# Order of the S5 output products inside a slot of a two-layer decoder trunk

## The chip, the cores and the metric

The kernel runs on one core of a Trainium2 chip. The metric is the device time of one execution in microseconds (us). Three runs of the kernel before gave 893.55, 893.63 and 894.71 us; their median, 893.63 us, is the time before. One further execution was profiled, and every row shown here is from that one.

Engine names are those of the profile: PE is TensorE's matmul side and PEld its weight loads, DVE is VectorE, ACT ScalarE, POOL GpSimd, and SP the queue that issues most transfers. SPq, ACTq and POOLq are the queues that issue DMAs.

## The reference

The reference is a causal decoder trunk of two layers over 256 positions of width 2048, in float32. Each layer is a normalisation, a large input projection, two kinds of sequence mixer side by side, a gate, and an output projection; a last normalisation follows. The first layer mixes with dilated attention and gated linear attention (GLA), the second with an S5 state-space layer and a gated linear recurrence (HGRN2).

What matters here is S5. Its 1024 channels are 64 groups of 16, each with a complex diagonal state of 64:

```
bu_re = einsum('gph,sbgh->sbgp', bb_re, ut);  bu_im = einsum('gph,sbgh->sbgp', bb_im, ut)
x_re, x_im = associative_scan over the positions, with the decay a_re, a_im
y = einsum('ghp,sbgp->bsgh', c_re, x_re) - einsum('ghp,sbgp->bsgh', c_im, x_im) + d_skip * ug
y = gelu(y);  return y * sigmoid(y @ w_glu + b_glu)
```

## The kernel before

**The projections.** Almost all of the time is weight projections. Each weight block of 512 columns comes from memory in groups of 1 MB (`raw`, three buffers, line 144). `load_split` (line 143) splits each half group into a rounded part `wh` on ACT (line 168) and a remainder `wl` on DVE (line 169), with three buffers each. `gemm_fm` (line 181) and `gemm_tm` (line 200) then issue three products for every 128 rows: high by high, high by low, low by high. A half group is 24 matmuls of 256 columns, or 12 of 512. The loads, `wh` and `wl` have raised priority.

**Slots.** After each half group `hook()` (line 135) takes one entry of the list `fillq` and issues its functions directly behind the last projection matmul. So S5's small matmuls stand between the half groups of the HGRN2 projections. S5 is done in four quarters (`s5_quarter`, line 552), each with eleven slots (line 651): two slots of input products with the scan, some empty ones, one in which the next quarter's input is loaded, and two slots of output products.

**A quarter.** `v_mm` (line 574) issues the input products: 64 rows by 64 columns, for two halves `g` of the partitions (matmul line 583). DVE multiplies them with tables (lines 589 to 592), scans (lines 603 and 604), and writes two results: the tile `X` (line 611, one instruction for each half `g`) and then the tile `t2`, which is `t["t"][1]` (line 612). `y_mm` (line 614) makes the output in one bank `py` of PSUM. For each of eight channel pairs `pr` there are two products over 128 rows of `X` with the tables `PA` and `PB` (line 621), and two over 64 rows of `t2` with `Pi` (line 625), which add into columns 1 to 63 of the same targets. The half `g` goes to partitions 64 g to 64 g + 63. A float32 product is two matmul instructions in the trace, so a slot of four pairs is 16 products and 32 instructions, 16 from each line. `finish` (line 631) copies `py` out on ACT (line 633), sends it to memory and back in another layout (lines 636 and 639; four of the eight writes are issued by ACT, four by POOL), and applies the gelu (lines 641 to 649).

**What sets the order.** The program is written in one order, and a planner with a model of the engines' times (`schedule_with_timeline_sim=True`, line 1124) turns it into a fixed order for each engine ahead of the run. It may place an instruction between others when its inputs come late in the model. Products into one PSUM bank stay in the order of the program. On the chip each engine takes its list in order and waits on semaphores. `SP` issues the `raw` loads and the loads of `X` from one queue (lines 157 and 567); `X` has two buffers, so a new load of `X` waits until line 621 has read the old one.

Of the kernel before, what the change touches and what calls it, by code (L numbers as in the profile page):

```python
# [57 lines left out]
def trunk(ctx: ExitStack, tc: tile.TileContext, I, out):  # L58
    nc = tc.nc
    V, G, A, T = nc.vector, nc.gpsimd, nc.scalar, nc.tensor  # L60
# [29 lines left out]
    def pm_tile(name="pm"):  # L90
        return pm.tile([128, 512], F32, name=name, tag="pm")
# [162 lines left out]
    gs = small.tile([128, 8], F32, name="gs")  # L254
# [297 lines left out]
    def s5_quarter(qt):  # L552
        t = {}
# [20 lines left out]
        def v_mm(h, n):  # L574
            def go():
                if n == 0:
                    t["pv"] = pm_tile().rearrange("p (w r c) -> p w r c", w=2, r=4)
                pv, X = t["pv"], t["X"]
                for w in range(2):
                    for pr in range(2 * n, 2 * n + 2):  # L580
                        for g in range(2):
                            us = slice(64 - g * 64, 128 - g * 64)
                            T.matmul(pv[g * 64:g * 64 + 64, w, pr], t["W"][w][us, 4 * h + pr],
                                     X[us, g, 4 * h + pr], start=True, stop=True)
                if n == 1:
                    hs = slice(4 * h, 4 * h + 4)
                    Rc, Rs, _ = t["R"]
                    t1, t2, t3, t4 = t["t"]
                    V.tensor_mul(t1[:, hs], pv[:, 0], Rc[:, hs])
                    V.tensor_mul(t4[:, hs], pv[:, 0], Rs[:, hs])  # L590
                    V.tensor_mul(t2[:, hs], pv[:, 1], Rs[:, hs])
                    V.tensor_mul(t3[:, hs], pv[:, 1], Rc[:, hs])
            return go
# [17 lines left out]
                V.tensor_sub(t["X"][gs, g, :, 1:64], t1[gs, :, 0:63], t3[gs, :, 0:63])  # L611
            V.tensor_add(t2, t2, t4)

        def y_mm(pr):
            def go():
                if pr == 0:
                    t["py"] = pm_tile().rearrange("p (r c) -> p r c", r=8)
                py, X = t["py"], t["X"]
                PA, PB, Pi = t["P"]
                for g, w in enumerate((PA, PB)):  # L620
                    T.matmul(py[g * 64:g * 64 + 64, pr], w[:, pr], X[:, g, pr], start=(pr == 0), stop=False,  # L621
                             skip_group_check=True)
                for g in range(2):
                    gs = slice(g * 64, g * 64 + 64)
                    T.matmul(py[gs, pr, 1:64], Pi[gs, pr], t["t"][1][gs, pr, 0:63], start=False, stop=True,  # L625
                             skip_group_check=True)
                if pr == 7:
                    finish()
            return go

        def finish():
            ys = sp_.tile([128, 8, 64], F32, name="ys")
            A.activation(ys, t["py"], AF.Copy)
            for g in range(2):
                for s in range(4):
                    (nc.gpsimd if s % 2 else nc.scalar).dma_start(
                        yv[g, s][:, 8 * qt:8 * qt + 8], ys[g * 64 + s * 16:g * 64 + s * 16 + 16])
            yc = sp_.tile([128, 2, S], F32, name="yc")
            nc.gpsimd.dma_start(yc, s5_y[256 * qt:256 * qt + 256].rearrange("(j p) f -> p j f", p=128))
            gw = sp_.tile([128, 2, S], F32, name="gw")  # L640
            A.activation(gw, yc, AF.Square)
            A.activation(gw, gw, AF.Copy, scale=0.044715, bias=1.0)
            V.tensor_mul(gw, gw, yc)
            A.activation(gw, gw, AF.Tanh, scale=math.sqrt(2.0 / math.pi))
            A.activation(yc, yc, AF.Copy, scale=0.5)
            for n in range(2):
                V.scalar_tensor_tensor(oT[:, 2 * qt + n].rearrange("p (c s) -> p s c", s=4),
                                       gw[:, n].rearrange("p (s c) -> p s c", s=4), 1.0,
                                       yc[:, n].rearrange("p (s c) -> p s c", s=4), op0=OP.add, op1=OP.mult)

        return load0, [[load1, v_mm(0, 0), v_mm(0, 1)], [v_mm(1, 0), v_mm(1, 1), scan], [], [], None, [], [], []] + [[y_mm(4 * n + m) for m in range(4)] for n in range(2)] + [[]]

    quarters = [s5_quarter(qt) for qt in range(4)]
    quarters[0][0]()
    for qt in range(4):
# [94 lines left out]
    for half in range(2):  # L750
# [8 lines left out]
        for g in range(2):  # L759
# [3 lines left out]
            for n in range(2):  # L763
                k0 = 8 * g + 4 * n
                if half:
                    w, l = xh[:, k0:k0 + 4], xl[:, k0:k0 + 4]
                else:
                    w = stream.tile([128, 4, 256], F32R, name="wh", bufs=3)
# [368 lines left out]
```

## Time and profile before

| | |
|---|---|
| median of three runs | 893.63 us (893.55 to 894.71) |
| the profiled execution | 892.18 us, of which its span, first to last instruction, is 890.4 us |
| PE busy | 874.7 us, 98% of the span, 7728 matmuls |
| DVE, ACT busy | 635.5 us (71%), 472.0 us (53%) |
| mean granted clock of TensorE | 0.995 of full speed |

A busy share is an average over the whole span. Matmuls are pipelined, so the end of one is modelled and the starts are the firmer numbers: the time that a run of matmuls takes is read from the start of its first to the start of what follows it.

### The profile page before, as it was taken

The page shows a single profiled execution, that of the slowest core. Times are in us where ns is not written, and L with a number is a line of the kernel's source. Part 1 is how long each engine was busy: PE and PEld are TensorE (multiplying, and loading weights), DVE is VectorE, ACT ScalarE, POOL GpSimd, SP SyncE. Part 2 cuts the span into 40 slices and gives each one's busy share as a digit, 9 for nine tenths or more (in the row PEclk, how much of TensorE's full clock was granted, in tenths as well). Part 3 has the DMA queues.
Part 4 walks back from the last instruction along what each step waited for, and adds up shares of the span by engine and source line. Part 5 has one row for each costly group of instructions (what it writes and reads, how often), then busy time and mean ns, then how long its engine had stood idle before and what let it go on. Part 6 is the DMA issues. An engine that isn't in the chain of part 4 may idle for free.

```text
span 890.4 us, 18689 instructions
## 1 busy us (share of the span) xinstructions
PE 874.7 (98%) x7728; PEld 802.0 (90%) x7728; DVE 635.5 (71%) x1197; ACT 472.0 (53%) x715; POOL 54.4 (6%) x106
## 2 busy tenths in 40 slices
PE   8999999999999999999999999999999999999995
PEld 8987899889998899999999998799877899988894
DVE  7988975989869858756675677676987756665562
ACT  7654546665645765645543335355545475444451
POOL 0001100111101101000000001100110000000000
PEclk9999999999999999999999999999999999999998
DMA  9827743777656555555576566744643544544532
GB/s 317 316 102 218 259 160 146 237 256 251 220 204 230 205 190 196 197 200 199 200 283 222 206 230 198 260 172 167 225 166 139 206 190 172 202 180 177 179 132 94
DMA packets 40388, 180.40 MB, mean 203 GB/s; under 512 B 12720, under 2 KB 14256, under 8 KB 22768
## 3 DMA queue, kind: packets, MB, share of 16 engines
q1 hardware_dynamic: 29440, 154.99, 49.2%
q0 software_dynamic: 7984, 22.69, 7.5%
q10 hardware_dynamic: 2880, 1.54, 0.6%
q8 instruction: 60, 0.98, 0.4%
q14 instruction: 24, 0.20, 0.1%
HBM read 166.48 MB, written 12.71 MB: 201 GB/s over the span
## 4 chain that ended last, share of the span: by engine, by line
PE 81%; DVE 6%; DMA 4%; ACT 4%; issue 3%; SPq 0%; POOL 0%; ACTq 0%; POOLq 0%; DVEq 0%
PE pg L181 47%; PE pg L200 24%; DMA raw<-in_w_dram 2%; PE pg L756 2%; DVE wl L169 2%; PE pm L287 1%; PE pm L339 1%; DMA E<-ed 1%; ACT wh L168 1%; PE pm L621 1%; PE pm L625 1%; PE pm L308 1%; PE pm L415 1%; PE pm L1025 1%; ACT bb L1019 0%
## 5 line engine op out<-in xcount | busy, mean ns | idle before, releaser
L168 ACT ACTIVATE wh<-raw 128x1024 fp32r<-128x1024 f32 (+2 forms) x276 | 287.7, 1046 | 325.4 <-PE pg L181 193.7
L169 DVE TENSOR_TENSOR wl<-raw,wh 128x1024 fp32r<-128x1024 f32 (+2 forms) x276 | 332.0, 1206 | 167.9 <-ACT wh L168 163.1
L181 PE MATMUL pg<-xh,wh 128*128 128x256 f32 x1024 | 161.8, 279 | 2.2 <-ACT wh L168 2.2
L181 PE MATMUL pg<-xh,wl 128*128 128x256 f32 x1024 | 163.2, 280 | 0.4 <-DVE wl L169 0.4
L181 PE MATMUL pg<-xl,wh 128*128 128x256 f32 x1024 | 161.2, 278 | 0.0
L181 PEld LDWEIGHTS pg<-xh,wh 128*128 128x128 f32 x1024 | 136.7, 188 | 3.8 <-ACT wh L168 3.2
L181 PEld LDWEIGHTS pg<-xh,wl 128*128 128x128 f32 x1024 | 137.0, 188 | 1.6 <-DVE wl L169 0.8
L181 PEld LDWEIGHTS pg<-xl,wh 128*128 128x128 f32 x1024 | 136.7, 188 | 0.6 <-issue 0.3
L200 PE MATMUL pg<-wl,xh 128*128 128x512 f32 x320 | 100.9, 396 | 0.6 <-DVE wl L169 0.6
L200 PE MATMUL pg<-wh,xl 128*128 128x512 f32 x320 | 100.7, 394 | 0.0
L200 PE MATMUL pg<-wh,xh 128*128 128x512 f32 x320 | 100.2, 394 | 0.0
L200 PEld LDWEIGHTS pg<-wl,xh 128*128 128x128 f32 x320 | 59.0, 188 | 14.2 <-DVE wl L169 1.4
L200 PEld LDWEIGHTS pg<-wh,xl 128*128 128x128 f32 x320 | 59.8, 188 | 12.8
L200 PEld LDWEIGHTS pg<-wh,xh 128*128 128x128 f32 x320 | 59.3, 188 | 12.8
L181 PE MATMUL pg<-yh,wh 128*128 128x256 f32 x320 | 50.0, 277 | 0.0
L181 PE MATMUL pg<-yl,wh 128*128 128x256 f32 x320 | 49.5, 277 | 0.0
L181 PE MATMUL pg<-yh,wl 128*128 128x256 f32 x320 | 49.5, 277 | 0.0
L181 PEld LDWEIGHTS pg<-yh,wh 128*128 128x128 f32 x320 | 42.6, 188 | 0.0
L181 PEld LDWEIGHTS pg<-yl,wh 128*128 128x128 f32 x320 | 42.4, 188 | 0.0
L181 PEld LDWEIGHTS pg<-yh,wl 128*128 128x128 f32 x320 | 42.4, 188 | 0.0
L965 POOL DMA_DIRECT2D tabs<-pc x44 | 23.8, 547 | 162.3 <-DVE x L975 42.5
L200 PE MATMUL pg<-wh,yh 128*128 128x512 f32 x96 | 30.1, 395 | 0.0
(350 smaller groups left out, 1008.2 us busy)
## 6 DMA issues: line engine op xcount, KB each, us to landing
raw<-in_w_dram SPq DMA_DIRECT2D x100, 1024.0 KB, 4.9
raw<-in_wo_dram SPq DMA_DIRECT2D x28, 1024.0 KB, 4.8
tb<-tabs POOLq DMA_DIRECT2D x8, 768.0 KB, 6.9
tabs<-pc POOLq DMA_DIRECT2D x20, 256.0 KB, 5.5
raw<-in_wg_dram SPq DMA_DIRECT2D x4, 1024.0 KB, 4.8
raw<-in_wo1l_dram SPq DMA_DIRECT2D x4, 1024.0 KB, 4.8
raw<-in_w_dram SPq DMA_DIRECT2D x6, 512.0 KB, 7.9
tabs<-pc POOLq DMA_DIRECT2D x24, 128.0 KB, 4.6
```

Source lines behind the costliest of these rows:

```text
L168: state["wh"] = A.activation(w, r, AF.Copy)
L169: V.tensor_sub(l, r, w)
L181: state["mm"] = T.matmul(ps[:, c], w[:, cs], a[:, kt], start=(i == 0 and n == 0 and c % 2 == 0), stop=(i == last and n == 2), skip_group_c ...
L200: state["mm"] = T.matmul(ps[:, t], a[:, kt, ts_], w, start=(i == 0 and n == 0), stop=(i == last and n == 2), skip_group_check=True)
L287: T.matmul(ps[32 * b:32 * b + 32, t, hd], k[:, hd, r], Q[:, hd, r], start=True, stop=True)
L308: T.matmul(ps[j0:j0 + h, hd, j0 + h:j0 + 2 * h], k[:, hd, b:b + h], Qp[:, hd, b + h:b + 2 * h], start=True, stop=True)
L339: T.matmul(ps[:, (hd - h0) * dv:(hd - h0 + 1) * dv], AT[:, hd, t + j], v[:, j, hd * dv:(hd + 1) * dv], start=(j == 0), stop=(j == t))
L415: T.matmul(ps[:, t, 0:n], q[:, t * 128:(t + 1) * 128], k[:, 0:n], start=True, stop=True)
L621: T.matmul(py[g * 64:g * 64 + 64, pr], w[:, pr], X[:, g, pr], start=(pr == 0), stop=False, skip_group_check=True)
L625: T.matmul(py[gs, pr, 1:64], Pi[gs, pr], t["t"][1][gs, pr, 0:63], start=False, stop=True, skip_group_check=True)
L756: T.matmul(ps[:, t, 0:256], a_[:, kt, ts_], w_, start=(kt == 0 and n == 0), stop=(kt == KT - 1 and n == 2), skip_group_check=True)
L965: nc.gpsimd.dma_start(tabs[qt, dst, n], t[src].rearrange("p a b -> p (a b)"))
```

## The change

In a slot of the output, the eight products over 128 rows are issued first, for all four channel pairs, and then the eight over 64 rows. Before, the two kinds took turns, pair by pair. Products, operands, targets and start and stop flags are the same, and a slot's list now has one function in place of four.

```diff
-        def y_mm(pr):
+        def y_mm(n):
             def go():
-                if pr == 0:
+                if n == 0:
                     t["py"] = pm_tile().rearrange("p (r c) -> p r c", r=8)
                 py, X = t["py"], t["X"]
                 PA, PB, Pi = t["P"]
-                for g, w in enumerate((PA, PB)):
-                    T.matmul(py[g * 64:g * 64 + 64, pr], w[:, pr], X[:, g, pr], start=(pr == 0), stop=False,
-                             skip_group_check=True)
-                for g in range(2):
-                    gs = slice(g * 64, g * 64 + 64)
-                    T.matmul(py[gs, pr, 1:64], Pi[gs, pr], t["t"][1][gs, pr, 0:63], start=False, stop=True,
-                             skip_group_check=True)
-                if pr == 7:
+                for pr in range(4 * n, 4 * n + 4):
+                    for g, w in enumerate((PA, PB)):
+                        T.matmul(py[g * 64:g * 64 + 64, pr], w[:, pr], X[:, g, pr], start=(pr == 0), stop=False,
+                                 skip_group_check=True)
+                for pr in range(4 * n, 4 * n + 4):
+                    for g in range(2):
+                        gs = slice(g * 64, g * 64 + 64)
+                        T.matmul(py[gs, pr, 1:64], Pi[gs, pr], t["t"][1][gs, pr, 0:63], start=False, stop=True,
+                                 skip_group_check=True)
+                if n == 1:
                     finish()
             return go
...
-        return load0, [[load1, v_mm(0, 0), v_mm(0, 1)], [v_mm(1, 0), v_mm(1, 1), scan], [], [], None, [], [], []] + [[y_mm(4 * n + m) for m in range(4)] for n in range(2)] + [[]]
+        return load0, [[load1, v_mm(0, 0), v_mm(0, 1)], [v_mm(1, 0), v_mm(1, 1), scan], [], [], None, [], [], []] + [[y_mm(0)], [y_mm(1)], []]
```

## Rows read from the trace of the kernel before

**Rows 1.** The page: busy time and share of each engine, the clock that TensorE was granted in 40 slices of the span (9 is 90% or more), and the shares of the chain of work that ended last, by engine.

```profile
PE 874.7 (98%) x7728; PEld 802.0 (90%) x7728; DVE 635.5 (71%) x1197; ACT 472.0 (53%) x715; POOL 54.4 (6%) x106
...
PEclk9999999999999999999999999999999999999998
...
PE 81%; DVE 6%; DMA 4%; ACT 4%; issue 3%; SPq 0%; POOL 0%; ACTq 0%; POOLq 0%; DVEq 0%
```

**Rows 2.** The view of waits, PE alone, over the whole span: who waited for whom, us in total, times, the longest.

```profile
PE pg L181 <- ACT wh L168: 2.2, 3, 0.9
...
PE pg L200 <- DVE wl L169: 0.6, 2, 0.3
```

**Rows 3.** The same view from 500 to 700 us, for ACT.

```profile
ACT wh L168 <- PE pg L181: 47.9, 23, 4.0
ACT wh L168 <- PE pg L200: 20.3, 11, 4.4
```

**Rows 4.** The groups of instructions, shapes kept apart: line, engine, operation, tiles, rows * columns of the array, shape, count | busy us, mean ns of one | idle before.

```profile
L621 PE MATMUL pm<-X,tb 128*64 128x64 f32 x128 | 11.4, 246 | 0.0
L625 PE MATMUL pm<-t,tb 64*64 64x63 f32 x128 | 10.6, 242 | 0.0
...
L621 PEld LDWEIGHTS pm<-X,tb 128*64 128x64 f32 x128 | 6.7, 134 | 3.5 <-issue 1.4
...
L1025 PEld LDWEIGHTS pm<-PP,bb 128*64 128x64 f32 x128 | 4.2, 138 | 1.3 <-ACT wh L168 0.7 <-ACT junk L344 0.3
```

**Rows 5.** The timeline of PE in the first output slot of the first quarter: start us, us, engine, line, operation, tiles, rows * columns, shape, count of neighbours merged into the row. The rows left out go on in turns.

```profile
527.46 0.34 PE L621 MATMUL pm<-X,tb 128*64 128x64 f32 x4
527.73 0.33 PE L625 MATMUL pm<-t,tb 64*64 64x63 f32 x4
527.99 0.34 PE L621 MATMUL pm<-X,tb 128*64 128x64 f32 x4
...
529.31 0.33 PE L625 MATMUL pm<-t,tb 64*64 64x63 f32 x4
529.57 0.74 PE L181 MATMUL pg<-xh,wh 128*128 128x256 f32 x4
```

**Rows 6.** The timeline of PE at two places where small matmuls of one shape stand in a row: 32 of S5's table products over 128 rows (line 1025, in the preparation), and 32 and 64 of its input products over 64 rows (line 583), each with the projection matmuls behind them.

```profile
150.86 1.15 PE L1025 MATMUL pm<-PP,bb 128*64 128x64 f32 x32
151.94 0.39 PE L181 MATMUL pg<-xh,wl 128*128 128x256 f32 x1
...
503.12 1.15 PE L583 MATMUL pm<-X,tb 64*64 64x64 f32 x32
504.19 0.74 PE L181 MATMUL pg<-xh,wh 128*128 128x256 f32 x4
...
616.16 2.08 PE L583 MATMUL pm<-X,tb 64*64 64x64 f32 x64
618.18 0.75 PE L181 MATMUL pg<-xh,wl 128*128 128x256 f32 x4
```

**Rows 7.** The timeline of PE at the beginning of the output slots of the second, third and fourth quarter, where other work stands between the first products.

```profile
566.28 0.34 PE L621 MATMUL pm<-X,tb 128*64 128x64 f32 x4
...
567.86 0.33 PE L625 MATMUL pm<-t,tb 64*64 64x63 f32 x4
...
633.40 0.33 PE L621 MATMUL pm<-X,tb 128*64 128x64 f32 x2
...
634.42 0.27 PE L625 MATMUL pm<-t,tb 64*64 64x63 f32 x2
...
657.10 0.33 PE L621 MATMUL pm<-X,tb 128*64 128x64 f32 x2
...
659.18 0.33 PE L625 MATMUL pm<-t,tb 64*64 64x63 f32 x4
```

**Rows 8.** The timeline of DVE: the instruction that writes `t2` (line 612) in each of the four quarters.

```profile
522.19 0.68 DVE L612 TENSOR_TENSOR t<-t,t 128x512 f32<-128x512 f32 x1
...
563.77 0.69 DVE L612 TENSOR_TENSOR t<-t,t 128x512 f32<-128x512 f32 x1
...
632.34 0.69 DVE L612 TENSOR_TENSOR t<-t,t 128x512 f32<-128x512 f32 x1
...
656.28 0.68 DVE L612 TENSOR_TENSOR t<-t,t 128x512 f32<-128x512 f32 x1
```

**Rows 9.** The timeline of PE: the two places between 500 and 740 us at which a projection waited for `wl`, with the wait and its releaser in brackets; and the half group before the first of them.

```profile
554.65 0.62 PE L200 MATMUL pg<-wl,xh 128*128 128x512 f32 x2
...
557.78 0.72 PE L200 MATMUL pg<-wl,xh 128*128 128x512 f32 x2 [0.21 <-DVE wl L169]
...
648.64 0.73 PE L200 MATMUL pg<-wl,xh 128*128 128x512 f32 x2 [0.34 <-DVE wl L169]
```

**Rows 10.** The timelines of DVE and ACT around these places: the `wl` of 554.65 us; the first table product of the fourth quarter, with DVE's wait before it; and ACT's two waits for the transfer of `yc`.

```profile
553.25 1.20 DVE L169 TENSOR_TENSOR wl<-raw,wh 128x1024 fp32r<-128x1024 f32 x1
...
638.94 0.42 DVE L589 TENSOR_TENSOR t<-pm,tb 128x256 f32<-128x256 f32 x1 [1.49 <-PE pm L583]
...
550.90 0.64 ACT L641 ACTIVATE gw<-yc 128x512 f32<-128x512 f32 x1 [1.05 <-DMA yc<-s5y]
...
649.87 0.63 ACT L641 ACTIVATE gw<-yc 128x512 f32<-128x512 f32 x1 [1.59 <-DMA yc<-s5y]
```

**Rows 11.** The view of waits from 500 to 700 us, for the queue of SP.

```profile
SPq L567 <- PE pm L621: 12.5, 2, 7.4
```

## The prediction

> **What bounds the kernel now.** I read the page first. PE is busy for 98% of the span, DVE for 71%, ACT for 53%, and the chain of work that ended last is PE for 81% [rows 1]. Next the view of waits: over the whole span PE waits 2.2 us for ACT's `wh` in one kind of projection and 0.6 us for DVE's `wl` in the other [rows 2]. Seen from the other side, between 500 and 700 us, where all output slots lie, ACT waits 34 times and 68.2 us in all for PE to give back a buffer of `wh` [rows 3]: the supply of weights is mostly ahead of PE. So PE's own list is the bound, and a microsecond taken out of it should leave the total. The clock is granted in full in nearly every slice [rows 1], so no gain is to be looked for there.
>
> Then the timeline of PE in one output slot. The reader is to see how regular it is: the groups of four instructions from line 621 and of four from line 625 follow each other without a pause in the profile's busy time, and the next projection matmul begins at 529.57 us after a beginning at 527.46 us, 2.11 us for 32 instructions [rows 5]. That is 0.264 us for each of eight groups. Where 32 small matmuls of one shape stand in a row, they take 1.08 us over 128 rows (150.86 to 151.94 us) and 1.07 us over 64 rows (503.12 to 504.19 us); 64 of them take 2.02 us [rows 6]. The same number of instructions of the same size costs twice as much when the shape changes after every fourth. The mean durations hide this (246 and 242 ns, [rows 4]), since matmuls overlap; only the distance of starts shows it.
>
> **The change, part by part.** *The price of one turn.* From 32 to 64 instructions of one shape is 0.95 us, so a further instruction in a row costs 0.95 / 32 = 0.030 us [rows 6]. Four cost 0.12 us, and a group of four with its change of shape costs 0.264 us [rows 5]: a turn costs 0.145 us.
>
> *The new slot.* It is one group of 16 over 128 rows and one of 16 over 64. A group of 16 is bounded from two sides: a group of four with its turn plus twelve more instructions, 0.264 + 12 x 0.030 = 0.62 us, or the 32 in a row less sixteen, 1.07 - 16 x 0.030 = 0.59 us. Two groups are 1.18 to 1.24 us, and the slot gets 0.87 to 0.93 us shorter. I take 0.88, near the first, since its group of four is these very instructions. It is also six turns fewer at 0.145 us.
>
> *Eight slots.* There are 128 instructions from each of the two lines [rows 4], 32 in a slot, so eight slots: 8 x 0.88 = 7.0 us, and 7.0 to 7.4 by the two bounds. The places where other work stands between the first products need a count of their own [rows 7]. Before, the second quarter has the four instructions of the first pair alone and the other fourteen groups or so later; the third and fourth have the first product of half 0 alone, and the rest later. Counted as groups of one shape the quarters have 16, 16, 17 and 17, together 66. With the new order each needs four, and the third and fourth probably one more, because the first product waits for one half of `X` and the others for both: 18. So 48 turns go, 48 x 0.145 = 7.0 us, the same as by slots.
>
> *The wait for `t2`.* The first product over 64 rows now stands behind eight products over 128 rows, not behind two. PE reaches it some 12 x 0.030 = 0.36 us later after the slot's beginning, and `t2` has been there before: its instruction ended at 522.87, 564.46, 633.03 and 656.96 us [rows 8], and line 625 began at 527.73 [rows 5], 567.86, 634.42 and 659.18 us [rows 7], that is 4.9, 3.4, 1.4 and 2.2 us later. No new stall is expected; if the cover went, the whole rest of PE's list would be queued behind line 625. I cost this at nothing.
>
> *What is moved on other engines.* No instruction and no transfer is added. SP waits 12.5 us in two waits for line 621 before it may load a new `X` [rows 11], and the `raw` loads stand behind it in the same queue. Since line 621 now ends before the last products of line 625, SP goes on 0.6 us before the slot ends, and earlier by what the slots have saved. ACT's copy of `py` waits for the last product of line 625, which stays last. So both are released earlier, never later.
>
> *What does not come along.* Two places are tight already. At 557.78 and 648.64 us PE waits 0.21 and 0.34 us for `wl`, and the `wl` that ended at 554.45 us (553.25 + 1.20) was used at 554.65 us [rows 9, 10]. Ahead of them DVE works off the scan of a quarter between the splits, and PE reaches them 1.76 us earlier (two slots) than before. DVE starts these scans when the input products of the quarter are done, which also move. At the later place DVE was waiting 1.49 us for these products [rows 10] and can use no more than that, so 1.76 - 1.49 = 0.27 us comes back as a wait of PE. The other thing in the way is ACT: it stands 1.05 and 1.59 us for the transfer of `yc` [rows 10] ahead of the next `wh`. That transfer starts from the end of the output slots, so it moves too, unless its queue is held by `raw` loads. If it did not move at all, ACT would stand there 1.76 us longer, and with 0.20 us of cover at 554.65 us PE would lose up to 1.6 us in each of the two places, 3.2 us in all; at the lower end nothing. I take a give-back of 0.3 us, near the lower end, as the first cause alone has a row for its size.
>
> *The sum.* 7.0 - 0.3 = 6.7 us less. For a profiled execution that is 892.18 - 6.7 = 885.5 us with a span of 883.7. The median of three runs stands 1.45 us above the profiled execution, and the difference carries over: 893.63 - 6.7 = 886.9 us.
>
> **Rivals.**
>
> *The supply takes part of it.* As bounded above, the transfer of `yc` may not come earlier, and DVE, which is nearly always busy around the two waits, may end first there. That gives back up to 3.2 + 0.3 = 3.5 us and a time of 890.1 us. For it: the waits of rows 9. Against it: 68.2 us of ACT waiting for PE in the same stretch [rows 3].
>
> *The groups are cut up again.* The planner may put other work of another shape between the products, or the order may not survive into PE's list. Then the turns stay and the time is 893.6 us. Against it: in all four quarters the products of a slot stand in the program's order in the trace before, and apart from their beginnings they are in one piece [rows 5, 7].
>
> *The planner moves the output slots ahead of the scan (slower).* The plan is made anew from a changed program. If the slots of every quarter were placed two half groups earlier relative to DVE's scan, PE would arrive 5.8 us earlier (a half group is 2.9 us, from 554.65 to 557.78 us less the wait of 0.21 [rows 9]), and against the covers of 4.9, 3.4, 1.4 and 2.2 us it would wait 0.9 + 2.4 + 4.4 + 3.6 = 11.3 us: 893.63 - 7.0 + 11.3 = 897.9 us. With one half group it is 1.5 + 0.7 = 2.2 us of waits and a time of 888.8. It is slower than before from between one and two half groups on. For it: in two quarters the cover is small. Against it: the number and size of the instructions in a slot do not change, so a model of their times has little reason to move a slot that far.
>
> *Weight loads that don't overlap (slower).* Eight products over 128 rows in a row load weights into the same rows of the array each time. If a load had to wait for the matmuls in flight, a pair would cost 134 + 246 = 380 ns [rows 4], a slot 8 x 0.38 + 0.61 = 3.65 us in place of 2.11, and the time would be 893.63 + 8 x 1.54 = 905.9 us. Against it: line 1025 has the same shape in a row, and its 32 loads of 138 ns [rows 4], 4.4 us together, stand within 1.08 us [rows 6]; they must overlap. The Trainium skill has such a rule, in "TensorE: Matmul & The Clock Gate", Part 3, "The mechanism": a weight load overlaps matmuls in flight only when its group of rows differs. By that rule this rival would be the forecast; by the rows of line 1025 it is not.
>
> **How the numbers follow.** What a measurement of this kernel can tell from no change is about 0.2%, 1.8 us. My forecast has a chance of 0.70. The supply rival has 0.15, and it is faster by more than 1.8 us over its whole stretch. The planner's rival has 0.03 with one half group, still faster, and 0.04 with two, slower. Loads that don't overlap have 0.02, slower. Groups cut up again have 0.06, no change. So faster 0.70 + 0.15 + 0.03 = 0.88, the same 0.06, slower 0.06. The forecast's own range is 886.2 (7.4 us, nothing given back) to 887.8; the low end goes to 885.4, since the two waits of rows 9 (0.55 us) could go too if the plan falls well, and the high end to 890.6, which takes in the supply rival and leaves out about 0.12.
>
> **What would show it right or wrong.** In the timeline of PE an output slot must have two groups, of 16 instructions each, and take 1.18 to 1.24 us from the first of line 621 to the projection matmul behind it. The busy time of PE must fall by about 6 to 7 us with its share near 98%. The waits of PE for `wl` should be 0.6 to 1 us in total; 3 us or more there, or under the transfer of `yc` in ACT's waits, is the supply rival. A wait of PE at line 625 for line 612 is the planner's. If a slot stays at 2 us with the groups in the new order, the price of a turn, which I take from other lines of the same shapes, is wrong, and the prediction with it.

## The result, and the profile after

The changed kernel takes 889.11 us (median of 20 runs, 885.8 to 894.61) beside 894.5 us for the kernel before (median of 20 runs too, one of them an outlier of 3954.35 us that a median hardly feels). The medians are 5.4 us apart. The ratio is 0.9936 with an interval of 0.9922 to 0.9951, that is 5.7 us less, with 4.4 to 7.0 us inside the interval. The forecast was 6.7 us less and 886.9 us. The sign is right, the time lies inside the range, and 0.9 us of the 2.2 us between forecast and median come from the kernel before, whose median is 894.5 us here against 893.63 us when the forecast was made.

The slots first. The timeline of PE in the second output slot of the first quarter, columns as in [rows 5]:

```profile
533.77 0.50 PE L181 MATMUL pg<-xh,wl 128*128 128x256 f32 x3
534.21 0.69 PE L622 MATMUL pm<-X,tb 128*64 128x64 f32 x16
534.82 0.68 PE L627 MATMUL pm<-t,tb 64*64 64x63 f32 x16
535.43 0.74 PE L181 MATMUL pg<-xh,wh 128*128 128x256 f32 x4
```

Two groups of 16 instead of eight of four [rows 5], and from 534.21 to the projection behind at 535.43 us it is 1.23 us. (Lines 622 and 627 are the 621 and 625 of before; everything behind them has moved by two.) The other unbroken slots take the same 1.226 us. Summed over every stretch of output products in the four quarters, from the start of the matmul ahead of a stretch to the start of the matmul behind it, it is 19.61 us before and 12.58 us after: 7.04 us less. (Without the steps into the stretches it is 17.09 and 10.06 us, 7.03 us less.)

The page of the profiled execution nevertheless says that its span is longer, 892.7 us against 890.4:

```profile
PE 874.1 (98%) x7728; PEld 804.5 (90%) x7728; DVE 636.0 (71%) x1197; ACT 473.1 (53%) x715; POOL 54.4 (6%) x106
...
PEclk9999999999999999999999999999999999999998
...
PE 74%; DVE 8%; ACT 6%; DMA 5%; issue 5%; SPq 0%; POOL 0%; POOLq 0%; DVEq 0%; ACTq 0%
```

PE's busy time fell by 0.6 us, not by 6 to 7 [rows 1]. This execution is the longest of the 20 (894.61 us), so its span alone says nothing; it has to be cut at a point that both kernels pass. The first input product of S5 (line 583) is such a point: nothing that the change touches stands before it, and up to there PE, ACT, DVE and POOL do the same instructions in the same order in both traces. Before, it begins at 503.12 us [rows 6]. After:

```profile
509.86 0.86 PE L583 MATMUL pm<-X,tb 64*64 64x64 f32 x22
```

It begins 6.74 us later, in a stretch that the change does not touch. From there to the end it is 890.4 - 503.12 = 387.28 us before and 892.7 - 509.86 = 382.84 us after: 4.44 us less. So in this execution 7.04 us went from the slots and 2.6 us came back behind them. The view of waits, PE over the whole span, shows the larger part (columns as in [rows 2]):

```profile
PE pg L200 <- ACT wh L168: 1.8, 1, 1.8
...
PE pg L200 <- DVE wl L169: 0.4, 2, 0.2
```

The single wait of 1.8 us for `wh` is new in this kind of projection. With the waits for `wl` it makes 2.2 us, against 0.6 before [rows 2]: 1.6 us come back here. It stands just ahead of the fourth quarter's slots. The timelines of PE, ACT and POOL around it:

```profile
653.78 0.62 PE L200 MATMUL pg<-wl,xh 128*128 128x512 f32 x2
656.17 0.74 PE L200 MATMUL pg<-wh,xh 128*128 128x512 f32 x2 [1.77 <-ACT wh L168]
```

```profile
644.81 1.06 ACT L672 ACTIVATE gk<-gf 128x1024 f32<-128x1024 f32 x1
645.78 1.99 ACT L168 ACTIVATE wh<-raw 128x1024 fp32r<-128x1024 f32 x2
653.88 0.63 ACT L643 ACTIVATE gw<-yc 128x512 f32<-128x512 f32 x1 [6.11 <-DMA yc<-s5y]
655.08 1.99 ACT L168 ACTIVATE wh<-raw 128x1024 fp32r<-128x1024 f32 x2
```

```profile
640.01 2.15 POOL L638 DMA_DIRECT2D s5y<-ys  x4
650.87 0.72 POOL L641 DMA_DIRECT2D yc<-s5y  x1 [8.72 <-DMA s5y<-ys]
```

ACT does two `wh` and then stands 6.11 us for `yc`; the next `wh` starts at 655.08 and PE, which needs it, goes on at 656.17. In the trace before the same wait of ACT was 1.59 us [rows 10], and three `wh` stood between the writes of `y` and that wait, not two. POOL's own queue before:

```profile
639.36 2.15 POOL L636 DMA_DIRECT2D s5y<-ys  x4
646.83 0.72 POOL L639 DMA_DIRECT2D yc<-s5y  x1 [5.32 <-DMA s5y<-ys]
```

From POOL's first write of `y` to the load of `yc`, which waits for all the writes to land, it is 10.86 us instead of 7.47. In the second traces below it is 11.35 and 7.99 us.

The remaining 1.0 us is in the projections themselves. The start-to-start distance of line 181's matmuls has two values in these traces, and each holds for long stretches. The timeline of PE at 760 us, before and then after:

```profile
760.02 0.62 PE L181 MATMUL pg<-xl,wh 128*128 128x256 f32 x4
760.47 0.62 PE L181 MATMUL pg<-xh,wl 128*128 128x256 f32 x4
```

```profile
759.95 0.63 PE L181 MATMUL pg<-xl,wh 128*128 128x256 f32 x4
760.42 0.64 PE L181 MATMUL pg<-xh,wl 128*128 128x256 f32 x4
```

Four matmuls take 0.453 us in the one and 0.471 us in the other, 113.4 and 117.8 ns each, at the same granted clock of 1.00. Summed over the 1211 steps of line 181 behind the first input product, what lies over 113.4 ns is 0.95 us before and 1.95 us after. With that the stretch adds up to the 0.1 us in which spans and waits are given: -7.04 + 1.6 + 1.0 = -4.4 us. Ahead of the first input product the same sum is 1.96 us before and 6.98 us after, which is 5.0 of the 6.74 us by which this execution came late to S5.

### The profile page after: what moved, and what is told of

It reads as the page before. It is cut to its first block, busy times and chain, and to the rows that moved or that the text cites. A ratio compares the mean times of both kernels' runs of the same rounds, so it can differ in the third digit from the quotient of the medians.

```text
span 892.7 us, 18688 instructions
## 1 busy us (share of the span) xinstructions
PE 874.1 (98%) x7728; PEld 804.5 (90%) x7728; DVE 636.0 (71%) x1197; ACT 473.1 (53%) x715; POOL 54.4 (6%) x106
## 4 chain that ended last, share of the span: by engine, by line
PE 74%; DVE 8%; ACT 6%; DMA 5%; issue 5%; SPq 0%; POOL 0%; POOLq 0%; DVEq 0%; ACTq 0%
PE pg L181 48%; PE pg L200 17%; DVE wl L169 2%; PE pg L758 2%; DMA tabs<-pc 2%; ACT wh L168 1%; PE pm L287 1%; DMA E<-ed 1%; PE pm L339 1%; DMA s5y<-ys 1%; ACT bb L1021 1%; DMA raw<-in_w_dram 1%; ACT x L1039 1%; PE pm L308 1%; DVE PP L1005 1%
## 5 line engine op out<-in xcount | busy, mean ns | idle before, releaser
L181 PE MATMUL pg<-xl,wh 128*128 128x256 f32 x1024 | 163.8, 280 | 0.0
```

The lines of the kernel that those rows point to most:

```text
L181: state["mm"] = T.matmul(ps[:, c], w[:, cs], a[:, kt], start=(i == 0 and n == 0 and c % 2 == 0), stop=(i == last and n == 2), skip_group_c ...
```

## The experiments

Times are medians beside runs of the kernel before on the same chip. "The stretch" is the time from the first input product to the end of the span in the profiled execution: 387.28 us before, 382.84 us after.

**The changed kernel and the kernel before, a second trace of each.** No edit.

> The changed kernel once more, for a second trace. Both theories of the price (change of shape, or adding into a target just written) expect output slots of 1.23 us and a time 0.5 to 0.8% below before. Theory A of the trace: the steps between the projection matmuls of line 181 have two rhythms, 113.4 and 117.8 ns, drawn anew in each execution; then this trace has slow stretches at other places or of another total length, and time less 4.4 ns for every slow step is within 2 us of the first trace's (about 894.6 - 8.1 = 886.5 us). Theory B: the changed order brings them; then the long slow stretches from 365 to 464 us and from 744 to 788 us stand there again. The wait of 1.8 us for ACT in the fourth quarter: if it comes from the transfer of yc landing late in that one execution, it is gone or has another size; if the plan makes it, it is there again with 1.5 to 2 us.

> The kernel before once more, for a second trace. Slots of 2.10 us. If the wait of PE in the fourth quarter belongs to the changed kernel, PE waits under 0.5 us there, as in the first trace (0.34), and ACT waits under 2 us for the transfer of yc of the third quarter (1.59). If the slow rhythm of line 181 from 742 to 787 us, which stands in all five traces with a changed order, belongs to them too, it is missing here; if it is drawn by lot, it may stand here.

The changed kernel: 889.68 us, ratio 0.9919 (0.9887 to 0.9951). The slots take 1.226 us again. The wait of PE for `wh` is there again, 2.29 us, behind a wait of ACT for `yc` of 6.64 us, so it belongs to the changed kernel's plan and not to one execution. The slower rhythm between 365 and 464 us, 99 us long in the first trace, is gone, and the one between 742 and 788 us is there again. The stretch is 384.84 us: here the fourth quarter's slots themselves came out longer, under a clock that fell soon behind the end of the wait at 652.72 us. Windows of that trace: start:end, us, busy time of PE (count), PEld, DVE, ACT, POOL, then granted clock, DMA share, GB/s.

```profile
652.00:653.00 1.00, 0.28 (x1) 0.28 (x2) 0.75 (x2) 1.00 (x2) 0.00 (x0) 1.00 0.34 139
653.00:655.00 2.00, 2.00 (x26) 1.43 (x25) 2.00 (x4) 2.00 (x4) 0.00 (x0) 0.88 0.00 0
655.00:656.00 1.00, 1.00 (x7) 0.45 (x6) 1.00 (x2) 0.61 (x1) 0.00 (x0) 0.50 0.00 0
656.00:659.00 3.00, 3.00 (x51) 2.68 (x51) 2.18 (x6) 0.26 (x1) 0.00 (x0) 0.68 0.62 224
```

0.50 is the lower of the two levels, 1.2 of 2.4 GHz. The last 48 products of the quarter take 2.69 us there and 1.84 us in the first trace. The kernel before: 892.5 us for one run, slots of 2.10 us, no wait for `wh` in line 200, the stretch 387.46 us against 387.28. So the cut at the first input product repeats within 0.2 us for the kernel before, while its spans of 890.4 and 890.7 us happen to agree as well.

**Groups of two pairs.** Four products over 128 rows, then four over 64 rows, and the same again: four groups of eight instructions in a slot.

```diff
-                for pr in range(4 * n, 4 * n + 4):
...
-                for pr in range(4 * n, 4 * n + 4):
...
+                for p0 in range(4 * n, 4 * n + 4, 2):
+                    wide(p0)
+                    wide(p0 + 1)
+                    narrow(p0)
+                    narrow(p0 + 1)
```

> Groups of two channel pairs: four products over 128 rows, four over 64, twice in a slot, so four groups where before has eight and the change has two. If a change of shape is the price (0.146 us each): a slot of 4 x 0.264 + 16 x 0.030 = 1.53 us, 4.7 us less in all than before, 2.3 us more than the change. If the price is adding into a target that was written just before: already here four products lie between a target and what adds into it, so the slot is near 1.23 us.

889.75 us, ratio 0.9946 (0.9924 to 0.9969). A slot is 1.52 us (531.76 to 533.27):

```profile
531.76 0.45 PE L623 MATMUL pm<-X,tb 128*64 128x64 f32 x8
532.14 0.45 PE L629 MATMUL pm<-t,tb 64*64 64x63 f32 x8
532.51 0.45 PE L623 MATMUL pm<-X,tb 128*64 128x64 f32 x8
532.90 0.45 PE L629 MATMUL pm<-t,tb 64*64 64x63 f32 x8
533.27 0.51 PE L181 MATMUL pg<-xh,wh 128*128 128x256 f32 x2
```

`wide` and `narrow` are the loops over `g` of the one and the other kind. Two changes of shape more than the changed kernel cost (1.518 - 1.226) / 2 = 0.146 us each, and six more cost (2.11 - 1.226) / 6 = 0.147 us in the kernel before [rows 5]. The price is one for each change, as the prediction has it.

**The old order with one shape.** The order pair by pair is back, but the second products run over all 128 rows. Each half then adds the other half's states too, so `y` is not the kernel's.

```diff
...
-                        T.matmul(py[gs, pr, 1:64], Pi[gs, pr], t["t"][1][gs, pr, 0:63], start=False, stop=True,
+                        T.matmul(py[gs, pr, 1:64], Pi[:, pr], t["t"][1][:, pr, 0:63], start=False, stop=True,
...
+                for pr in range(4 * n, 4 * n + 4):
+                    wide(pr)
+                    narrow(pr)
```

> The order of before, pair by pair, but the second kind of product takes all 128 rows, as the first does (this leaves the values of y out of account: each half also adds the other half's states). Alternation and the distance between a target and what adds into it are those of before, only the shape no longer changes. If the change of shape is the price: a slot of 32 instructions in a row, 1.08 us, 8 x 1.03 = 8.2 us less than before. If adding into a target just written is the price: still 2.1 us a slot and no gain.

887.25 us, ratio 0.9923 (0.9899 to 0.9947). Eight groups of four in turns, with no price at all (the rows left out go on in turns):

```profile
527.73 0.34 PE L623 MATMUL pm<-X,tb 128*64 128x64 f32 x4
527.89 0.28 PE L629 MATMUL pm<-t,tb 128*64 128x63 f32 x4
528.01 0.29 PE L623 MATMUL pm<-X,tb 128*64 128x64 f32 x4
...
528.81 0.38 PE L181 MATMUL pg<-xh,wh 128*128 128x256 f32 x1
```

1.08 us, in the order of before. Each second product adds into the target that the product before it has just written, and that costs nothing. It is the change of shape alone that is paid for.

**Turns kept, addition far from its product.** The products over 64 rows of one half slot stand between the 128-row products of the next.

```diff
...
+                if n == 0:
+                    for pr in range(4):
+                        wide(pr)
+                else:
+                    for pr in range(4):
+                        wide(pr + 4)
+                        narrow(pr)
+                    for pr in range(4, 8):
+                        narrow(pr)
```

> The first slot has the products over 128 rows of pairs 0 to 3; the second alternates those of pairs 4 to 7 with the additions of pairs 0 to 3, and the additions of pairs 4 to 7 come last. No addition follows its target's product closely, but the shapes alternate: 9 groups a quarter, where before has 16 and the change has 4. If the change of shape is the price: 9 x 0.264 + 28 x 0.030 = 3.2 us a quarter for both slots (0.62 and 2.6), against 4.2 before and 2.45 with the change, so 4 us less than before in all. If adding into a target just written is the price: 2.45 us a quarter or less, 7 us less than before.

891.06 us, ratio 0.9955 (0.9932 to 0.9977). The two slots of a quarter take 0.615 + 2.570 = 3.19 us, as the price of a turn says (3.2), not the 2.45 of two groups. This is the other side of the run before: with distance to the target, but with turns, the price stays.

**The table load behind the writes of `y`.** In the third quarter the load of the next quarter's tables stands in POOL's queue right ahead of the writes.

```diff
-            t["P"] = tab(2, 3)
+            with tc.issue_after(state["yw"].ins) if qt else ExitStack():
+                t["P"] = tab(2, 3)
...
-                    (nc.gpsimd if s % 2 else nc.scalar).dma_start(
+                    state["yw"] = (nc.gpsimd if s % 2 else nc.scalar).dma_start(
```

> The change, with the load of the next quarter's output tables (768 KB) issued behind the writes of y, where it stood ahead of them; the rest of the orders stays. If the writes land late because that load and a weight load go ahead of them, the time from the last write to the load of yc in the third quarter falls from 8.2 and 8.9 us to 5 to 7 us, ACT's wait for yc falls from 6.1 and 6.6 us to 3 to 4 us, PE's wait behind it from 1.8 and 2.3 us to under 0.6 us, and the time is 2 us below the change. If the weight load alone does it, these numbers stay within 1 us of what they were, and so does the time.

888.34 us, ratio 0.9934 (0.9913 to 0.9954). ACT still waits 6.6 us for `yc` and PE 1.9 us for `wh`. The expected 2 us did not come: from POOL's first write to the load of `yc` it is 10.71 us with the table load behind the writes, beside 10.86 with it ahead. The table load is not what holds the writes up.

**The gelu's first three steps on POOL.** If ACT does not stand for `yc`, its `wh` come in time.

```diff
-            A.activation(gw, yc, AF.Square)
-            A.activation(gw, gw, AF.Copy, scale=0.044715, bias=1.0)
-            V.tensor_mul(gw, gw, yc)
+            G.tensor_mul(gw, yc, yc)
+            G.tensor_scalar(gw, gw, 0.044715, 1.0, op0=OP.mult, op1=OP.add)
+            G.tensor_mul(gw, gw, yc)
```

> The change, with the first three operations of the gelu on POOL, so that ACT's first wait for the result comes behind three splits of the third quarter's end, not two. If PE's wait in the fourth quarter comes from wh standing behind ACT's wait for yc, it falls to under 0.5 us although yc lands as late as before (8 us or more from the last write to the load), and the time is 2 us below the change. If yc's landing does not matter and the supply is late by itself, PE's wait stays at 1.8 us or more.

894.63 us, ratio 1.0005 (0.9987 to 1.0023): all of the gain is gone. PE's waits between 500 and 700 us:

```profile
PE pg L200 <- DVE wl L169: 2.7, 3, 2.0
PE pm L287 <- DVE gk L325: 2.5, 1, 2.5
PE pm L627 <- DVE t L612: 1.1, 1, 1.1
PE pg L200 <- ACT wh L168: 0.4, 1, 0.4
```

The wait for `wh` fell to 0.4 us as expected, but the plan made for this program brings 6.3 us of others, and behind the two longest of them PE ran at a mean granted clock of 0.54 (555 to 558 us) and 0.53 (596 to 599 us). So this run doesn't price the wait. It shows something else: DVE's `t2` can come late to the products over 64 rows, 1.1 us here, and a new plan can cost what the slots have saved.

**All 32 products of a quarter in one slot.** Sixteen over 128 rows, then sixteen over 64, in the second of the two slots.

```diff
...
+                for pr in range(8):
+                    wide(pr)
+                for pr in range(8):
+                    narrow(pr)
+                finish()
...
-        return load0, [[load1, v_mm(0, 0), v_mm(0, 1)], [v_mm(1, 0), v_mm(1, 1), scan], [], [], None, [], [], []] + [[y_mm(0)], [y_mm(1)], []]
+        return load0, [[load1, v_mm(0, 0), v_mm(0, 1)], [v_mm(1, 0), v_mm(1, 1), scan], [], [], None, [], [], []] + [[], [y_mm(0)], []]
```

> All 16 products over 128 rows of a quarter, then all 16 over 64, in one slot: two groups where the change has four. If turns and the passage from and to the projections cost what the traces show (0.146 us a turn, about 0.2 us for one passage less), a quarter takes 2.16 us in place of 2 x 1.23 and saves 0.5 us with the passage: 2 us in all below the change. If the longer slot only moves a wait, or the wait in the fourth quarter grows, the time is that of the change within 1 us.

893.19 us, ratio 0.998 (0.9962 to 0.9999). The slot is 2.16 us for a whole quarter, as expected, and the output products of all quarters take 10.44 us, 9.2 less than before. The time does not follow, because PE reaches a half group of the second quarter before DVE has its `wl`:

```profile
556.12 0.62 PE L200 MATMUL pg<-wh,xl 128*128 128x512 f32 x2
559.94 1.22 PE L200 MATMUL pg<-wl,xh 128*128 128x512 f32 x2 [3.20 <-DVE wl L169]
```

With 1.27 us more for `wh` in the fourth quarter, 4.5 us come back at two places. The wait of 3.20 us does not come from an earlier PE. Counted from the first input product, PE is ready for this matmul 0.5 us earlier than in the changed kernel, but its `wl` ends 3.0 us later (52.56 against 49.56 us). The delay begins on ACT in the first quarter. It stands 5.48 us at its last write of `y`, which its list has ahead of two splits, and DVE waits 5.32 us for the first of them:

```profile
539.14 6.43 ACTq L644 DMA_DIRECT2D s5y<-ys  x2
545.68 2.01 ACT L168 ACTIVATE wh<-raw 128x1024 fp32r<-128x1024 f32 x2 [5.48 <-DMA s5y<-ys]
```

The clock then takes more: from 560 to 565 us it was granted at 0.50, and the matmuls behind the wait took about 3 us longer than at 1.00. With these 3 us, the two waits and the rhythm of line 181 (1.0 us) the stretch, 0.9 us shorter than before, adds up to within 0.2 us. So the supply takes back nearly all here, but by way of the writes of `y`, and neither branch of the expectation has this time.

**`yc` without its way through memory.**

```diff
-                    (nc.gpsimd if s % 2 else nc.scalar).dma_start(
+                    yw = (nc.gpsimd if s % 2 else nc.scalar).dma_start(
...
-            nc.gpsimd.dma_start(yc, s5_y[256 * qt:256 * qt + 256].rearrange("(j p) f -> p j f", p=128))
+            with tc.issue_after(yw.ins):
+                nc.gpsimd.dma_start(yc, s5_u[256 * qt:256 * qt + 256].rearrange("(j p) f -> p j f", p=128))
```

> The changed kernel, with the load of yc taken from the other scratch tensor (the S5 input, written long before) and held only behind the issue of the last of POOL's writes of y. It leaves out the way of y through memory: the gelu works on the S5 input in place of y, so the output is not the kernel's. Theory A (the 1.8 to 2.3 us for which PE waits at the beginning of the fourth quarter's slots come from ACT standing 6 us for yc, whose load waits for the writes to land): ACT's wait for yc in the third quarter falls from 6.1 us to 3 us or less, PE's wait for wh at 650 to 656 us falls to 0.4 us or less, the slots of the fourth quarter take 1.23 us, and the time falls by 1.5 to 2 us, to about 887.3 us. Rival B (the splits behind are late by themselves, since DVE is busy throughout and releases raw late): PE still waits 1 us or more for wh or wl at that place and the time stays at 889.

886.48 us, ratio 0.9924 (0.9907 to 0.9941); the stretch is 381.17 us. Between 600 and 720 us PE has no wait at all. ACT does not stand for `yc` in the third quarter:

```profile
640.00 0.62 ACT L644 ACTIVATE gw<-yc 128x512 f32<-128x512 f32 x1
```

The theory expected 887.3 us. The rival (`wl` or `raw` late by themselves) is out: with `yc` early, the splits come in time. But the plan made for this program also has three `wh` ahead of this instruction, as before the change, where the changed kernel has two. So the run does not tell which of the two, the early `yc` or the third `wh`, takes the wait away.

**One shape in the changed order.** The second products over 128 rows on a table `PZ` whose other half is zero, so the sum is the same.

```diff
+        G.memset(PZ[64 - g * 64:128 - g * 64, g], 0.0)
...
+                nc.gpsimd.dma_start(PZ[gs, g].rearrange("p r e -> p (r e)"), tabs[qt, gs, 4])
...
-                        T.matmul(py[gs, pr, 1:64], Pi[gs, pr], t["t"][1][gs, pr, 0:63], start=False, stop=True,
+                        T.matmul(py[gs, pr, 1:64], PZ[:, g, pr], t["t"][1][:, pr, 0:63], start=False, stop=True,
```

> The changed order with the second products made over 128 rows too, on a table of Pi whose other half is zero (two tiles of 64 rows loaded by two transfers in place of one part of a wider one; ys and gw share a buffer to make room). It computes the same. No change of shape is left in a slot: a slot takes 1.08 us as in the version over all rows before, against 1.23, and the eight slots 0.7 to 1.2 us less than the changed kernel's 12.6. Theory A (the price is the change of shape, and what is lost behind depends on the plan): 888.4 us if the fourth quarter's wait of PE for wh stays at about 2 us, and 887 if the plan places ACT's wait for yc behind three wh again. Rival B (the extra transfers and the shared buffer hold up the tables or the gelu): PE waits for the tables at the products of line 628 (their number in this kernel) or the wait of ACT for yc gets longer than 6.6 us, and the time is 890 or more.

890.4 us, ratio 0.9954 (0.994 to 0.9967). The slots are 1.08 us as expected. The time is rival B's, but neither of its signs is there: PE does not wait for the tables, and ACT's longest wait for `yc` is 6.37 us, under the 6.6 it names. What PE waits for is `wh` (0.5 us), `wl` (1.0 us) and `t2` ahead of a second product (0.5 us, line 634), and 1.4 us stand at line 287 with no releaser in the profile. The last change of shape is worth 1.0 us in the slots, and more than that is lost in these waits. Whether the extra transfers and the shared buffer cause them or the new plan does is not shown.

**The gelu written later, with two plans.** The gelu is moved into slot 6 of the next quarter, or into slot 7 in the control, behind a later `wh`. The planner gives ACT three `wh` ahead of its wait for `yc` in the one and two in the other.

```diff
+        def gelu():
+            with tc.issue_after(state["wh"].ins):
+                A.activation(gw, yc, AF.Square)
...
+            slots[6].append(quarters[qt - 1][2])
```

> The changed kernel with the gelu of a quarter written two slots into the next quarter and held behind a later wh on ACT. It computes the same. In the planned order of ACT in the third quarter, one wh stands directly behind the copy to ys and two more behind it ahead of the first gelu instruction, three in all, against two in the changed kernel. Theory A (ACT stands for yc with too few wh done ahead, and that is the wait of PE in the fourth quarter): ACT still waits some 4 to 6 us for yc, but PE's wait for wh at 645 to 656 us falls from 1.8 or 2.3 to 0.5 us or less, and from the first input product (line 583) to the end of the span it takes 1.3 to 2 us less than the changed kernel's 382.84 and 384.84 us, about 381.5; the time is about 887.5. Rival B (DVE's wl or the raw loads are late by themselves): PE waits as long, for wl or wh, at the same place, and the stretch stays at 383 or more.

> The control to the kernel beside it: the gelu is written one slot later still, but the planner gives ACT in the third quarter two wh ahead of the first gelu instruction, as in the changed kernel. It computes the same. Theory A: PE waits about 2 us for wh in the fourth quarter, as in the changed kernel, and from the first input product to the end it takes 382.5 to 384.9 us. Rival B (what counts is how the gelu is written, not the order that the planner gives): it is like the kernel beside it.

887.59 us, ratio 0.992 (0.9891 to 0.9949), and for the control 886.92 us, ratio 0.9917 (0.9888 to 0.9946). PE's waits from 600 to 720 us, first with three `wh` ahead, then the control:

```profile
PE pg L200 <- DVE wl L169: 0.4, 1, 0.4
PE pm L287 <- DVE gk L325: 0.3, 1, 0.3
```

```profile
PE pg L200 <- ACT wh L168: 1.9, 1, 1.9
PE pg L200 <- DVE wl L169: 0.5, 1, 0.5
```

The wait goes with three `wh` and stays with two. But the pair differs in a second point: POOL's load of `yc` goes out 6.68 us behind its first write in the one and 10.92 us in the control, and ACT stands 3.50 and 6.37 us for it. So the pair alone does not show that the order is the cause. The other traces part the two. One shape in the changed order has three `wh` and ACT's wait of the control, 6.37 us, and PE waits 0.54 us for `wh`, not 1.89. Groups of two pairs have two `wh` and a wait of ACT of 5.06 us, and PE does not wait for `wh` there:

```profile
650.93 0.63 ACT L650 ACTIVATE gw<-yc 128x512 f32<-128x512 f32 x1 [6.37 <-DMA yc<-s5y]
653.22 0.74 PE L200 MATMUL pg<-wh,xh 128*128 128x512 f32 x2 [0.54 <-ACT wh L168]
```

```profile
651.73 0.63 ACT L651 ACTIVATE gw<-yc 128x512 f32<-128x512 f32 x1 [5.06 <-DMA yc<-s5y]
```

In all seven traces with two `wh` PE's wait at this place grows with ACT's: none at 5.06 us, 0.75 at 5.81, 1.27 at 6.01, 1.77 at 6.11, 1.89 at 6.37 and 6.63, 2.29 at 6.64 us. So a late `yc` makes the wait, and a third `wh` ahead covers most of it.

The second half of the expectation failed: the stretch is 383.39 us, not 381.5, and the control with its wait is shorter, 380.78 us. Two differences can be read. The control has hardly any of line 181's slower steps (0.26 us over 113.4 ns, against 1.95). And the first has new gaps between 670 and 680 us. They come to some 1.4 us over the usual steps, besides the waits that the view above lists. The longest step among them, with the listed wait of 0.43 us in it, is this:

```profile
678.93 0.63 PE L200 MATMUL pg<-wh,xl 128*128 128x512 f32 x2
680.00 0.50 PE L200 MATMUL pg<-wl,xh 128*128 128x512 f32 x1 [0.43 <-DVE wl L169]
```

Neither of the two, nor any other version here, is told apart from the changed kernel by its interval as the better one.

## Why the prediction was right, and which term was off

**What bounds the kernel.** Right. PE's list is the bound: in the changed kernel what the slots save leaves the stretch, less waits and steps of PE that can be named. In the version with the gelu in slot 6 about 0.8 us stays without a name: its slots are 7.15 us shorter, 0.1 us of waits and 1.0 us of rhythm and 1.4 us of gaps come back, which leaves 4.65, and the stretch is 3.89 us shorter.

**The price of one turn.** 0.145 us predicted, 0.146 to 0.147 measured, from two other versions. That it is the change of shape, and neither the addition into a target just written nor the number of instructions, was an assumption taken from other lines [rows 6]. The old order with one shape (no price) and the turns with far targets (full price) show it.

**The new slot and the eight slots.** 1.18 to 1.24 us and 7.0 us less; measured 1.226 and 7.04. A row of 16 like instructions could be worked out from rows of 32 and 64.

**The wait for `t2`.** Nothing predicted, none in the changed kernel. The cover is not safe, though: 0.5 and 1.1 us appear in two versions with other plans.

**What does not come along.** This is the term that was mis-sized: "I take a give-back of 0.3 us, near the lower end, as the first cause alone has a row for its size." In the profiled execution 1.6 us came back as waits. The first cause, DVE's splits, gave nothing; PE's waits for `wl` were 0.6 us before and 0.4 us after (0.7 in the second trace). The second cause, bounded at 1.6 us in each of two places, came near one of them: 6.6 us behind the second wait for `wl` (0.34 us before, 0.22 after) PE waits 1.77 us for `wh`, or 2.29 in the second trace. The prediction let the transfer of `yc` move with the slots "unless its queue is held by `raw` loads", and took the low end. It moved the other way: 10.86 us instead of 7.47 from the first write to the load. ACT's order mattered too, which no row of before could show, since the plan is made anew: one `wh` fewer stands ahead of the wait. In the run without the way through memory and in the plan with three `wh` PE's wait at this place is gone, but both have an earlier `yc` and a third `wh`; the traces compared there show that both count. What makes the writes land later in the changed kernel is not settled. The table load was excluded. A `raw` load of 1 MB that meets the writes is the candidate. SP issues it when DVE has read the buffer (its largest wait there is for `wl`, line 169), not when PE comes. After the change it is issued 0.5 us ahead of the end of ACT's copy of `py` (639.72 us), before the change 2.5 us ahead of it (639.07 us):

```profile
639.19 0.33 SPq L157 DMA_DIRECT2D raw<-in_w_dram  x1
```

```profile
636.60 0.33 SPq L157 DMA_DIRECT2D raw<-in_w_dram  x1
```

The other traces agree: with the `raw` load 3.8 us ahead of the copy's end the load of `yc` goes out 7.0 us behind that end, with 2.5 us 7.8 and 8.3, with 1.1 us 9.1 and 10.0, and with 0.7 us or less 10.2 to 11.6 us. That is a correlation; no run moved the `raw` load alone.

**A term that the sum lacked.** 1.0 us came back in the rhythm of line 181 behind the slots. It is in ten of the twelve traces of versions with another order or shape and in neither trace of the kernel before, but the gelu on POOL and the control of the last pair don't have it. So it goes with the fall of the plan, and it is not shown that the order of the products causes it.

**The sum and the rivals.** -6.7 predicted, -5.4 measured by medians (-7.0 to -4.4), -4.44 in the stretch of one execution. By the medians alone forecast and supply rival (890.1) are not told apart; by the signs that the prediction names they are. PE's busy time did not fall by 6 to 7 us in this execution, since 6 us of slower steps hide it, so that sign was a bad one. ACT's wait for `yc` was the supply rival's, and that rival is what happened, near one place of its two. Its sign has to be read place by place: from 500 to 720 us ACT's four waits for `yc` come to 9.5 us before and 9.4 after, and only the one ahead of the fourth quarter's slots grew. The groups were not cut up again, `t2` was not late, and 16 weight loads into the same rows, 137 ns each on the mean, fit into a group of 0.61 us, so the other three rivals are out. The last of them was also priced too low: a slot has sixteen weight loads over 128 rows (128 in eight slots, [rows 4]), not eight, so by its own terms a slot would have taken 16 x 0.38 + 0.61 = 6.7 us. And the low end of the range lies 0.3 us under its own terms, 886.2 - 0.55 = 885.7 us. The rule of the Trainium skill weighed there ("TensorE: Matmul & The Clock Gate", Part 3, "The mechanism"), by which such loads wait for the matmuls in flight, is not borne out by these rows.

## What to carry to other kernels

Where small matmuls of two shapes take turns, read the distance of starts, not the mean duration, and price each change of shape; group by shape or give both one shape. Then look at what PE arrives at earlier: a transfer that begins where the shortened work ends need not come earlier, and the engine that waits for it may carry the next weights in its list. And cut two traces at a point ahead of the change before comparing their spans.

## What the runs showed of the hardware that was not expected

Line 181's matmuls have two rhythms, 113.4 and 117.8 ns from start to start, at one granted clock, and keep one for up to 99 us. The same program had the slower one from 365 to 464 us in one trace and not in another. The effect on a span was up to 6 us, as large as the change itself. The switches between them fall on interruptions of the row, a slot or a short wait; what sets them is open.

The granted clock fell to 0.50 behind PE's wait of 2.29 us in one trace of the changed kernel, and stayed at 1.00 behind its wait of 1.77 us in the other:

```profile
656.00:658.00 2.00, 1.83 (x20) 1.27 (x22) 1.85 (x3) 2.00 (x4) 0.00 (x0) 1.00 0.28 107
```

So the price of a wait in this kernel can be more than its length: here the last 48 products behind it took 0.85 us longer. In the version with all products of a quarter in one slot the wait of 3.20 us was followed by some 3 us more.
